# VectorE, ScalarE and GpSimd in the program's own order through the mixer of a hybrid decoder layer

## The chip, the core and the metric

The kernel runs on one NeuronCore of a Trainium2 chip. The metric is the device time of one execution in microseconds (us), lower is better. Engines are named as in the profile: PE (TensorE matmuls), PEld (its weight loads), DVE (VectorE), ACT (ScalarE), POOL (GpSimd) and SP (SyncE, which here only issues DMAs).

## The reference

One layer of 2048 channels on 256 tokens. After an RMSNorm, one wide projection gives the inputs of two branches: a gated DeltaNet (GDN, 8 heads of 128) and a block-sparse attention (MoBA, 8 heads of 128; with 256 tokens it is plain causal attention). Both are merged by sigmoid gates; an output projection and a gated MLP of width 5632 follow.

```python
h = rms_norm(x, ln1)
qkv_a, beta_a, decay_a, z_a, qkv_b, gate_a, gate_b = split_columns(h @ w_in)
# branch A: silu(causal conv of width 4) on q, k, v; l2norm of q and k;
# decay g, beta; per chunk of 64 tokens a triangular solve and the delta rule;
# rms_norm(o) * silu(z)
y_a = gated_deltanet(qkv_a, ...) @ w_branch_a
# branch B: rotary on a quarter of the head, causal softmax attention
y_b = moba_attention(rope(q_b), rope(k_b), v_b) @ w_branch_b
x = x + (sigmoid(gate_a) * y_a + sigmoid(gate_b) * y_b) @ w_out
u = causal_dwconv(rms_norm(x, ln2) @ w_up, ffn_conv, ffn_conv_bias)
x = x + (silu(u_gate) * u_val) @ w_down
out = rms_norm(x, final_norm)
```

## The kernel before

**Weights in two parts.** A float32 matrix product is made of three fp32r products: high part of the weights by the high part of h, high by low, low by high. A weight tile is 128 x 2048 float32 (1 MB, tile `wraw`, three buffers, loaded by SP in `fetch`). `split` (line 137) turns each half of 1024 columns into `wh` (a cast on ACT) and `wl` (a subtraction on DVE, line 134). `wh` and `wl` have four buffers each, so two tiles' worth. `pump` makes halves in program order as far as `due` allows; `take` hands the next tile to the matmuls; `gone` says which tiles the matmuls have been written out for, so that their buffers can be taken again.

**Main matmuls.** `chunk` gives 256 output columns of the projection: two tiles of 16 blocks, three matmuls of 256 columns each, so 96 matmuls of `main_mm` (line 123); a half is read by 24 of them. In each group of two heads (four groups) the chunks are GDN q, k, v and z (`delta`), MoBA q and k (`queries`), and in every second group one product for the values (`values_of`). Then come 16 chunks of gates, the branch products, the output projection, the MLP. The first q and k of GDN are made ahead, in the load phase (line 296).

**Turns.** After some 16 main matmuls (`EVERY`) `main_mm` calls `tick`, which advances every generator in `bg` to its next `yield`: that is a turn. The generators are `gdn` (norms, decay factors, the solve, the state), `moba` (rotary, scores, softmax, values) and `rotary` (sine and cosine tables). They mix small matmuls, DVE, ACT and POOL work, and DMAs through DRAM tiles (`dA`, `dC`, `dX`, `dE`) that POOL issues.

**Convolution.** `conv4` (from line 498) writes `un = ps * R1b` with `join` (line 239), where `un` has one buffer for all convolutions, then one ACT scaling for each of two heads (line 506), six DVE multiply-adds (line 508) and a SiLU. For the first k `conv4` gets `mid`, which writes out `decay()` (lines 460 to 484, the per-head decay and beta) and places the six multiply-adds of that k behind decay's last scan (line 480).

**Order.** The tile framework schedules the whole program with a timeline model: each engine's instructions are put in an order of the model's choosing, by readiness and priority. `tc.issue_after(ins)` queues work behind one instruction of its engine (`late()` queues behind the last `wl` written out), `tc.high_priority()` (in `join`) moves work ahead. On the chip each engine then works through its list.

Of the kernel before, what the change touches and what calls it, by code (L numbers as in the profile page):

```python
# [72 lines left out]
def layer_kernel(ctx: ExitStack, tc: tile.TileContext, w_first, xT, pos, cst, vec, convw, ffw, bdv,  # L73
# [40 lines left out]
    def take():  # L114
        n = taken[0]
        taken[0] += 1
        due[0] = 2 * n + 3
        passed[0] = 0
        pump()
        return n, made[2 * n:2 * n + 2]  # L120

    def main_mm(ps, a, b, start, stop):
        mark[0] = pe.matmul(ps, a, b, start=start, stop=stop, skip_group_check=True).ins  # L123
        passed[0] += b.free_size()
        if passed[0] >= 6144:
            due[0] = 2 * taken[0] + 2
            pump()
# [82 lines left out]
    def block(ps, j, w, x, kt, k0=0, k1=None, turn=False):  # L210
        for k in range(k0, k1 or kt):
            wh, wl = cut(w, (k + (j * kt if kt == H else 0)) * P, P)
            for w_, a in ((wh, 0), (wh, 1), (wl, 0)):
                main_mm(ps[:, j], w_, x.one(k, a, turn), j == k == a == 0 and w_ is wh,
                        k == kt - 1 and w_ is wl)

    def chunk(x, kt, name, steps=((0, 0, None), (1, 0, None)), c=None):
# [9 lines left out]
        for i, (j, k0, k1) in enumerate(steps):  # L227
            if j not in ws:
                ws[j] = take()
            block(ps, j, ws[j][1], x, kt, k0, k1, bool(again) and name in ("gdn", "z", "moba"))  # L230
            if kt != H and j not in [t[0] for t in steps[i + 1:]]:
                gone.add(ws[j][0])
        if kt == H:
            gone.add(ws[0][0])
# [162 lines left out]
    def rotary():  # L397
# [89 lines left out]
    def turned(rem):  # L487
        pt = sdt("pt_cols")
        for i in range(2):
# [3 lines left out]
        for i in range(2):  # L493
            pe.transpose(pt[:, 80 + 16 * i:96 + 16 * i], R1[:16, i * P:(i + 1) * P], ident[:16, :16])
        dve.tensor_copy(cols.rearrange("p a b -> p (a b)"), pt[:, :112])
        dve.tensor_scalar(cols[:, 0:2, :].rearrange("p a b -> p (a b)"), pt[:, :32], -1.0, None, op0=ALU.mult)

    left, early = [], []

    def conv4(t, ps, b0, to=None, mid=None):  # L500
# [11 lines left out]
        else:  # L512
            act.activation(to, t.rearrange("p j (b c) -> p j b c", c=64), AF.Silu)

# [18 lines left out]
    def gdn(h0, kq, v):  # L533
# [4 lines left out]
        yield from wait(2)  # L538
        pq = sdt("ssq")[:, :P]
        with tc.issue_after(mark[0]):  # L540
            for c, (i, j) in enumerate(((0, 0), (0, 1), (1, 0), (1, 1))):
                pe.matmul(pq[32 * c:32 * c + 32], ones[:, :32], sq[:, j, i * P:(i + 1) * P], start=True, stop=True,
                          skip_group_check=True)
        act.copy(sq[:, 0, :P], pq)
        st = gl.tile([P, 8, 4], F32, name="st")

        def exps():
            dve.tensor_tensor(gam[:, :, 0::2, :], gam[:, :, 0:2, :], nm[:, None, None, :].to_broadcast([P, 2, 2, P]), op=ALU.add)
            for j in range(2):
                c = 8 + h0 + j  # L550
                for q, a in enumerate((0, 2, 1)):
                    act.activation(gam[:, j, q, :], gam[:, j, q, :], AF.Exp, bias=cols[:, a, c:c + 1])

        if h0:
            exps()
        yield

        pq = sdt("ssq")[:, :P]
        pe.transpose(pq, sq[:, 0, :P], ident)
        dve.tensor_scalar(st[:, 0, :], pq[:, ::32], EPS, P * EPS, op0=ALU.add, op1=ALU.mult)  # L560
# [3 lines left out]
        yield from wait(2)  # L564
# [5 lines left out]
        for j in range(2):  # L570
            mmg(p1[:, j], three(kqh[:, 0, j, P:], kql[:, 0, j, P:], kqh[:, :, j, P:], kql[:, :, j, P:]))
        yield
        if left:
            turned(left.pop())
        jk = g.tile([P, P], F32, name="jk", bufs=1)
        for j in range(2):
            for i, d in ((0, p0[j][:, 0, :P]), (1, p1[:, j, 0, :])):
                with late():
                    diag = dve.scalar_tensor_tensor(jk, d, 1.0, ident, op0=ALU.mult, op1=ALU.mult,
                                                    accum_out=st[:, 1, 2 * i + j:2 * i + j + 1])  # L580
# [4 lines left out]
        if not h0:  # L585
            with tc.issue_after(diag.ins):
                exps()
        aq0 = gl.tile([P, 2, 2, T], F32, name="aq0")
        aq1 = gl.tile([P, 2, 2, P], F32, name="aq1")
        for j in range(2):  # L590
            gv = gam[:, j, 0:2, :].rearrange("p a b -> p (a b)")
            dve.scalar_tensor_tensor(aq0[:, j], p0[j], st[:, 3, j:j + 1], gv[:, None, :].to_broadcast([P, 2, T]),
                                     op0=ALU.mult, op1=ALU.mult)
        for j in range(2):
# [3 lines left out]
        for i in range(2):  # L598
            for b in range(2):
                pe.transpose(pvt[:, 2 * i + b, :], v[:, 2 * i + b, :], ident)  # L600
        dA = dr.tile([4, P + 1, P], F32, name="dA")
        pool.dma_start(dA[0:2, :P].rearrange("j s c -> s j c"), aq0[:, :, 0, :P])
        pool.dma_start(dA[2:4, :P].rearrange("j s c -> s j c"), aq1[:, :, 0, :])
        dC = dr.tile([16, 32, 32], F32, name="dC")
# [5 lines left out]
        X = g.tile([P, 160], F32, name="X", bufs=1)  # L610
        pool.tensor_copy(X, C["rows"])
        yield
        rt2 = gl.tile([P, 2, 2], F32, name="rt2")
        vb = gl.tile([P, 2, 2, P], F32, name="vb")
        with tc.issue_after(highs[-1].ins):
            for j in range(2):
                for b in range(2):
                    o = slice(64 * b, 64 * b + 64)
                    act.activation(rt2[64 * j:64 * j + 64, :, b], st[o, 1, j::2], AF.Sqrt, bias=epst[o])
            for i in range(2):  # L620
                for b in range(2):
                    act.mul(vb[:, i, b], pvt[:, 2 * i + b], rt2[:, i, b:b + 1])
        yield from wait(13)
# [14 lines left out]
        Xr = g.tile([P, 16, 16], F32, name="Xr", bufs=1)  # L638
        pool.dma_start(Xr.rearrange("p m c -> p (m c)"), dram(dX, 0, (256, 16), (0, 8), (1, 256)))
# [9 lines left out]
        for q in range(4):  # L649
            pool.dma_start(S1[32 * q:32 * q + 32, :, 32 * q:32 * q + 32],  # L650
                           dram(dA, q * 64 * (P + 1) + 32, (P, 32), (2 * (P + 1) * P, 2), (1, 32)))
        yield from wait(10)
        with late():
            rows(Xm, W, Xr, False)
        for j in range(2):
            pool.dma_start(S2[64 * j:64 * j + 64, :, 64 * j:64 * j + 64],
                           dram(dA, j * (P + 1) * P + 64, (P, 64), (2 * (P + 1) * P, 2), (1, 64)))
# [3 lines left out]
        early.append(h0)  # L661
        E = gl.tile([P, 2, 2, 32], F32, name="E", bufs=1)
        pool.dma_start(E.rearrange("p e i c -> p (e i) c"), dram(dE, 0, (32, P), (4096, 4), (1, 32)))
        yield from wait(3)
        for q in range(4):
            for b in range(2):
# [4 lines left out]
        with late():  # L671
            dve.transpose(Et, E[:, 0])
        yield from wait(2)
        py = r3(sdt("py")[:, :64], 32)
        for i in range(2):
            pe.matmul(py[:, i], S1[:, i], Et[:, i], start=True, stop=True)
        Y = gl.tile([P, 2, 4, 32], F32, name="Y", bufs=1)
# [4 lines left out]
        for i in range(2):  # L682
            pe.matmul(pu[:, i], Y[:, i].rearrange("p a b -> p (a b)"), E[:, 1, i], start=True, stop=True)
        for j in range(2):
# [10 lines left out]
        for i in range(2):  # L695
            p0_ = sdt("w0")[:, :P]
            pe.matmul(p0_, UB[:, i, 0], vb[:, i, 0], start=True, stop=True)
            w0 = gl.tile([P, P], F32, name="w0", bufs=1)
# [4 lines left out]
            pe.matmul(pz, S2[:, i], w0, start=True, stop=True)  # L703
            dve.tensor_tensor(vb[:, i, 1], vb[:, i, 1], pz, op=ALU.subtract)
            yield from wait(2)
            p1_ = sdt("w1")[:, :P]
            pe.matmul(p1_, UB[:, i, 1], vb[:, i, 1], start=True, stop=True)
            apart(i, 1, p1_)
            yield
            if i == 0:  # L710
                pr = r3(sdt("r1"), P)
                for j in range(2):
                    pe.matmul(pr[:, j, :], aq0[:, j, 0, P:], u[:, j, :], start=True, stop=True)
                for j in range(2):
# [6 lines left out]
        for j in range(2):  # L721
            pe.matmul(po[:, j, :], aq0[:, j, 1, :P], u[:, j, :], start=True, stop=True)
            mmg(po[:, 2 + j, :], [(aq0[:, j, 1, P:], u[:, j, :]), (aq1[:, j, 1, :], u[:, 2 + j, :])])
        ot = gl.tile([P, 4, P], F32, name="ot", bufs=1)
        for p in range(4):
            act.activation(ot[:, p], po[:, p], AF.Square, accum_out=st[:, 4, p:p + 1])
        yield from wait(3)
        with late():
# [386 lines left out]
```

## Time and profile before

| | us |
|---|---|
| median of 3 runs | 1450.16 (1449.38 to 1450.17) |
| the profiled execution | 1450.27 |
| its span, first to last instruction | 1448.5 |

| engine | busy us | share of the span |
|---|---|---|
| PE | 1434.0 | 99% |
| PEld | 1377.9 | 95% |
| DVE | 951.4 | 66% |
| ACT | 771.9 | 53% |
| POOL | 186.3 | 13% |

The profiled execution lies within the spread of the three runs, so sums against its trace can be read against the median. Matmuls overlap, and the end of each is modelled: PE's busy time is no measure of its free time. Its waits, the spacing of its matmuls and the granted clock are.

### The profile page before, as it was taken

The numbers are of one execution on the slowest core, as the hardware profiler recorded it, in microseconds if no ns is written. First come the engines' busy times: TensorE is split into PE (matmuls) and PEld (weight loads), VectorE is DVE, ScalarE is ACT, GpSimd is POOL, SyncE is SP. The second block draws the span as 40 slices with busy tenths as digits, with TensorE's granted clock in tenths as the row PEclk, the third lists the DMA queues.
The fourth block names the chain that finished last, engine by engine and source line by source line (L and its number), as shares of the span: only waits on it lengthen the run. The fifth ranks groups of instructions, "written<-read, shape, count | busy, mean of one in ns | idle before, by whom it ended". The sixth has DMA issues, their size and how long they took to land.

```text
span 1448.5 us, 26964 instructions
## 1 busy us (share of the span) xinstructions
PE 1434.0 (99%) x11268; PEld 1377.9 (95%) x11268; DVE 951.4 (66%) x1385; ACT 771.9 (53%) x1095; POOL 186.3 (13%) x236
## 2 busy tenths in 40 slices
PE   9999999999999999999999999999999999999998
PEld 9989998999999999999999999999999998888886
DVE  7879577686755546767776666666666676555454
ACT  7676575665746444444555555554554554444444
POOL 0030221222203000101131111111111110000000
PEclk9999999999999999999999999999999999999999
DMA  8575554555555565566585555555555555555552
GB/s 315 191 230 188 188 171 168 183 201 190 165 176 181 194 204 185 195 228 215 198 278 190 202 189 191 203 188 191 202 185 195 202 182 198 196 187 200 193 188 113
DMA packets 46458, 283.81 MB, mean 196 GB/s; under 512 B 7632, under 2 KB 8800, under 8 KB 14464
## 3 DMA queue, kind: packets, MB, share of 16 engines
q1 hardware_dynamic: 39344, 270.38, 53.9%
q0 software_dynamic: 6272, 9.61, 2.5%
q8 instruction: 88, 1.44, 0.4%
q10 hardware_dynamic: 720, 2.10, 0.4%
q14 instruction: 34, 0.28, 0.1%
HBM read 275.34 MB, written 3.82 MB: 193 GB/s over the span
## 4 chain that ended last, share of the span: by engine, by line
PE 98%; ACT 1%; issue 0%; POOL 0%; DVE 0%; ACTq 0%; POOLq 0%
PE ps_up L123 33%; PE pd L88 17%; PE ps_gate L123 12%; PE ps_gdn L123 7%; PE ps_moba L123 6%; PE ps_wo L123 6%; PE ps_br L123 6%; PE ps_v L123 3%; PE ps_z L123 3%; PE ps_gdn L296 2%; PE g L88 1%; PE warm L283 0%; PE sc L766 0%; PE py_b L794 0%; PE po L88 0%
## 5 line engine op out<-in xcount | busy, mean ns | idle before, releaser
L134 DVE TENSOR_TENSOR wl<-wraw,wh 128x1024 fp32r<-128x1024 f32 (+1 forms) x496 | 611.4, 1234 | 373.1 <-ACT wh L137 370.0
L137 ACT CAST wh<-wraw 128x1024 fp32r<-128x1024 f32 (+1 forms) x496 | 515.7, 1043 | 581.8 <-PE ps_up L123 196.1
L123 PE MATMUL ps_up<-h,wh 128*128 128x256 f32 x2816 | 479.2, 276 | 0.0
L123 PEld LDWEIGHTS ps_up<-h,wh 128*128 128x128 f32 x2816 | 423.8, 188 | 0.0
L123 PE MATMUL ps_up<-h,wl 128*128 128x256 f32 x1408 | 388.9, 276 | 0.0
L123 PEld LDWEIGHTS ps_up<-h,wl 128*128 128x128 f32 x1408 | 264.4, 188 | 0.0
L123 PE MATMUL ps_gate<-hc,wh 128*128 128x256 f32 x1024 | 178.8, 278 | 0.0
L123 PEld LDWEIGHTS ps_gate<-hc,wh 128*128 128x128 f32 x1024 | 155.2, 188 | 0.0
L123 PE MATMUL ps_gate<-hc,wl 128*128 128x256 f32 x512 | 142.4, 278 | 0.0
L88 PE MATMUL pd<-wl,ah 128*128 128x512 f32 x336 | 125.4, 389 | 0.0
L88 PE MATMUL pd<-wh,al 128*128 128x512 f32 x336 | 124.4, 389 | 0.0
L88 PE MATMUL pd<-wh,ah 128*128 128x512 f32 x336 | 115.5, 389 | 0.0
L979 POOL TENSOR_TENSOR acts<-sg,cvf 128x256 f32<-128x256 f32 x44 | 62.7, 1425 | 408.2 <-ACT sg L978 399.2
L123 PE MATMUL ps_gdn<-hc,wh 128*128 128x256 f32 x640 | 113.5, 280 | 0.0
L123 PEld LDWEIGHTS ps_gdn<-hc,wh 128*128 128x128 f32 x640 | 97.6, 188 | 0.5 <-issue 0.4
L123 PEld LDWEIGHTS ps_gate<-hc,wl 128*128 128x128 f32 x512 | 96.4, 188 | 0.0
L123 PE MATMUL ps_moba<-hc,wh 128*128 128x256 f32 x512 | 92.4, 283 | 0.0
L123 PE MATMUL ps_gdn<-hc,wl 128*128 128x256 f32 x320 | 89.5, 280 | 0.0
L123 PE MATMUL ps_wo<-mc,wh 128*128 128x256 f32 x512 | 87.1, 276 | 0.0
L123 PEld LDWEIGHTS ps_moba<-hc,wh 128*128 128x128 f32 x512 | 79.2, 191 | 0.5 <-issue 0.4
L123 PEld LDWEIGHTS ps_wo<-mc,wh 128*128 128x128 f32 x512 | 77.2, 188 | 0.0
L88 PEld LDWEIGHTS pd<-wh,al 128*128 128x128 f32 x336 | 63.1, 188 | 13.2
(464 smaller groups left out, 1974.2 us busy)
## 6 DMA issues: line engine op xcount, KB each, us to landing
wraw<-in_w_up SPq DMA_DIRECT2D x88, 1024.0 KB, 4.9
wraw<-in_w_dn SPq DMA_DIRECT2D x44, 1024.0 KB, 4.9
wraw<-in_w_gate SPq DMA_DIRECT2D x32, 1024.0 KB, 4.9
wraw<-in_w_gdn SPq DMA_DIRECT2D x28, 1024.0 KB, 5.2
wraw<-in_w_moba SPq DMA_DIRECT2D x16, 1024.0 KB, 4.9
wraw<-in_w_o SPq DMA_DIRECT2D x16, 1024.0 KB, 5.0
wraw<-in_w_mv SPq DMA_DIRECT2D x8, 1024.0 KB, 4.9
wraw<-in_w_ba SPq DMA_DIRECT2D x8, 1024.0 KB, 4.9
```

The costliest lines, as they stand in the source:

```text
L88: pe.matmul(ps, a, b, start=(start and i == 0), stop=(stop and i == n - 1), **kw)
L123: mark[0] = pe.matmul(ps, a, b, start=start, stop=stop, skip_group_check=True).ins
L134: return (eng or dve).tensor_tensor(lo, src, hi.bitcast(F32), op=ALU.subtract)
L137: highs.append(act.copy(hi, src))
L296: pe.matmul(ps_two[b // 2][:, b % 2], wv[t][:, k - a, b * P:(b + 1) * P], hc.one(k, x_), start=(k == t == x_ == b % 2 == 0), stop=(k == KD ...
L979: pool.tensor_tensor(acts[:, c, :], sg, t[:, 1, :], op=ALU.mult)
```

## The change

- Between GDN's first v chunk and the end of the gates, DVE, ACT and POOL issue their instructions in the order in which the program writes them out (`tc.manual_schedule`). PE and SP stay with the scheduler; so does everything written out ahead of the region (the first q and k, `decay`) and behind it, and so does the place where the region's instructions fall among those.
- `late()` and the other `issue_after` uses inside the region go away.
- Convolutions from the first v on use `conv_turns`: `join` into `un` at once, then the ACT scalings, the multiply-adds of each head and the SiLU in turns of their own. The SiLU of z and the sigmoid of the gates come one turn later (`soon`).
- `gdn`, `moba` and `rotary` are cut into smaller portions, with a `yield` between what one engine makes and what the next reads, and whole turns between dependent DMAs.
- `gone` counts halves and no longer tiles, and `due` is one half further ahead, in all stages that use `pump`.

The diff, cut to its core:

```diff
@@ pump, take, main_mm
-            if n > 1 and n - 2 not in gone:
+            if n > 1 and (n - 2, h) not in gone:
...
-        due[0] = 2 * n + 3
+        due[0] = 2 * n + 4
...
-            due[0] = 2 * taken[0] + 2
+            due[0] = 2 * taken[0] + 3
@@ block
+            if (o + P) % HALF == 0:
+                gone.add((n, o // HALF))
@@ new, beside conv4 (which stays for the first q and k)
+    def conv_turns(t, ps, b0, to=None):
+        un = g.tile([P, 2, T], F32, name="un", bufs=1)
+        join(un, ps, R1b)
+
+        def turns():
+            yield
+            for j in range(2):
+                act.activation(t[:, j, :], un[:, j, :], AF.Identity, scale=cwv[:, b0 + j, 3:4])
+            yield
+            for j in range(2):
+                w = cwv[:, b0 + j, :]
+                for d in (1, 2, 3):
+                    dve.scalar_tensor_tensor(t[:, j, d:], un[:, j, :T - d], w[:, 3 - d:4 - d], t[:, j, d:],
+                                             op0=ALU.mult, op1=ALU.add)
+                yield
+            if to is None:
+                act.activation(t, t, AF.Silu)
+            else:
+                act.activation(to, t.rearrange("p j (b c) -> p j b c", c=64), AF.Silu)
+
+        bg.append(turns())
@@ delta
             else:
+                if gr == 0:
+                    order_st.enter_context(tc.manual_schedule(engines={
+                        mybir.EngineType.DVE, mybir.EngineType.Activation, mybir.EngineType.Pool}))
                 ps = chunk(hc, KD, "gdn")
...
-                conv4(t, ps, 8 * a + h0,
-                      v.rearrange("p b (j c) -> p j b c", c=64))
+                conv_turns(t, ps, 8 * a + h0, v.rearrange("p b (j c) -> p j b c", c=64))
...
-        act.activation(yv, yv, AF.Silu)
+        soon(lambda: act.activation(yv, yv, AF.Silu))
@@ gdn: solve and its DMAs
-        yield from wait(13)
...
-            with late():
-                dve.tensor_tensor(tm[:, :, :, :i + 1], Xd[:, :, :, :i + 1],
-                                  Ad[:, :, None, :i + 1, i].to_broadcast([P, 2, 2, i + 1]), op=ALU.mult)
+            dve.tensor_tensor(tm[:, :, :, :i + 1], Xd[:, :, :, :i + 1],
+                              Ad[:, :, None, :i + 1, i].to_broadcast([P, 2, 2, i + 1]), op=ALU.mult)
...
-            if i % 4 == 3:
+            if i % 3 == 2:
                 yield
...
-        yield from wait(10)
-        with late():
-            rows(Xm, W, Xr, False)
+        yield
+        Xr = g.tile([P, 16, 16], F32, name="Xr", bufs=1)
+        pool.dma_start(Xr.rearrange("p m c -> p (m c)"), dram(dX, 0, (256, 16), (0, 8), (1, 256)))
+        yield from wait(5)
+        rows(Xm, W, Xr, False)
+        yield
...
+        yield from wait(2)
         E = gl.tile([P, 2, 2, 32], F32, name="E", bufs=1)
         pool.dma_start(E.rearrange("p e i c -> p (e i) c"), dram(dE, 0, (32, P), (4096, 4), (1, 32)))
...
-        yield from wait(6)
+        yield from wait(2)
         Et = gl.tile([P, 2, 32], F32, name="Et", bufs=1)
-        with late():
-            dve.transpose(Et, E[:, 0])
+        dve.transpose(Et, E[:, 0])
         yield from wait(2)
         py = r3(sdt("py")[:, :64], 32)
@@ moba
-        yield from wait(3)
+        yield from wait(4)
...
+        largest(0)
+        yield
+        largest(1)
+        yield
+        exps(0)
+        exps(1)
+        yield from wait(2)
+        share(0)
+        yield
+        share(1)
+        yield from wait(2)
@@ the end of the region, after the gates
     while bg:
         tick()
+    order_st.close()
```

The rest of the diff is of the same kind: more `yield`s between a small matmul and the instruction that reads its result, `values_of` reading a half of a tile at a time, `turned` cut into a PE and a DVE part, `st` with three buffers.

## Rows read from the trace of the kernel before

**Rows 1.** The page: engines; then shares of the chain that ended last.

```profile
PE 1434.0 (99%) x11268; PEld 1377.9 (95%) x11268; DVE 951.4 (66%) x1385; ACT 771.9 (53%) x1095; POOL 186.3 (13%) x236
PE 98%; ACT 1%; issue 0%; POOL 0%; DVE 0%; ACTq 0%; POOLq 0%
```

**Rows 2.** The chain in order of time: start us, length us, what.

```profile
31.80 10.72 PE ps_gdn L123 x94
42.52 10.92 PE ps_z L123 x96
...
449.51 98.01 PE ps_gate L123 x864
```

**Rows 3.** PE's waits: line, waited for, us in total, times, longest.

```profile
PE py L676 <- issue: 5.0, 2, 4.3
PE pot L738 <- ACT ot L733: 1.4, 1, 1.4
```

**Rows 4.** Stretches: PE, PEld, DVE, ACT, POOL busy (count), granted clock, DMA.

```profile
252.00:253.00 1.00, 0.00 (x0) 0.00 (x0) 1.00 (x3) 1.00 (x2) 1.00 (x3) 0.74 0.99 410
...
255.00:256.00 1.00, 1.00 (x6) 1.00 (x7) 0.94 (x2) 0.00 (x0) 1.00 (x3) 0.50 0.11 17
...
258.00:259.00 1.00, 1.00 (x7) 1.00 (x7) 0.75 (x1) 0.00 (x0) 0.00 (x0) 0.50 1.03 418
...
260.00:261.00 1.00, 1.00 (x11) 1.00 (x11) 0.28 (x1) 0.40 (x1) 0.00 (x0) 1.00 0.94 377
```

**Rows 5.** Timeline ahead of the long wait: start, us, instruction [idle before <-releaser].

```profile
239.02 0.53 POOL L639 DMA_DIRECT2D Xr<-dX  x1 [2.47 <-DMA dX<-X]
239.87 1.05 ACT L137 CAST wh<-wraw 128x1024 fp32r<-128x1024 f32 x1 [1.80 <-PE ps_moba L123]
244.29 1.08 DVE L643 TENSOR_TENSOR tw<-W,Xr 128x512 f32<-128x512 f32 x1 [5.44 <-DMA Xr<-dX]
245.28 1.23 DVE L134 TENSOR_TENSOR wl<-wraw,wh 128x1024 fp32r<-128x1024 f32 x1
250.37 0.78 POOL L663 DMA_DIRECT2D E<-dE  x1 [1.35 <-DMA dE<-X]
254.23 0.25 DVE L672 STREAM_TRANSPOSE Et<-E 128x64 f32<-128x64 f32 x1 [0.31 <-DMA E<-dE]
```

**Rows 6.** Timeline of DVE and ACT from the first convolutions to v's join.

```profile
41.36 1.21 DVE L134 TENSOR_TENSOR wl<-wraw,wh 128x1024 fp32r<-128x1024 f32 x1
45.91 0.69 DVE L239 TENSOR_TENSOR un<-ps_gdn,R 128x512 f32<-128x512 f32 x1
47.65 0.40 DVE L463 SCALAR_TENSOR_TENSOR nz<-gc 16x256 f32<-16x256 f32 x1
51.88 0.42 ACT L464 ACTIVATE ez<-nz 16x256 f32<-16x256 f32 x1
52.32 0.28 DVE L468 TENSOR_SCALAR den<-ez 16x256 f32<-16x256 f32 x1 [0.50 <-ACT ez L464]
...
54.99 1.23 DVE L134 TENSOR_TENSOR wl<-wraw,wh 128x1024 fp32r<-128x1024 f32 x1 [0.61 <-ACT wh L137]
...
64.36 1.21 DVE L134 TENSOR_TENSOR wl<-wraw,wh 128x1024 fp32r<-128x1024 f32 x1
...
66.59 0.84 DVE L508 SCALAR_TENSOR_TENSOR kq<-un,cwv,kq 128x255 f32<-128x255 f32 x2
71.83 0.47 DVE L508 SCALAR_TENSOR_TENSOR kq<-un,cwv,kq 128x253 f32<-128x253 f32 x1
72.33 0.69 DVE L239 TENSOR_TENSOR un<-ps_gdn,R 128x512 f32<-128x512 f32 x1
```

**Rows 7.** Groups between 30 and 450 us: busy us, mean ns | idle before.

```profile
L134 DVE TENSOR_TENSOR wl<-wraw,wh 128x1024 fp32r<-128x1024 f32 x135 | 164.5, 1221 | 66.3 <-ACT wh L137 63.4 <-PE ps_z L123 2.3
L630 DVE TENSOR_TENSOR tm<-X,Xa 128x8 f32<-128x8 f32 (+14 forms) x60 | 13.3, 221 | 0.8
L632 DVE TENSOR_REDUCE X<-tm 128x4 f32<-128x8 f32 (+14 forms) x60 | 11.3, 188 | 0.8
```

More of the change, by code (lines that the diff above doesn't have):

```diff
@@ L226, in chunk @@
                 pe.matmul(idle[:, :P], ws[0][1][0][0][:, :P], x.one(0, 0)[:, :P], start=True, stop=True)
-        for i, (j, k0, k1) in enumerate(steps):
+        for j, k0, k1 in steps:
             if j not in ws:
                 ws[j] = take()
[L230 to L234, printed above, removed]
+            block(ps, j, ws[j], x, kt, k0, k1, bool(again) and name in ("gdn", "z", "moba"))
         return ps
@@ L563, in gdn @@
         split(kqh, kql, kq)
-        yield from wait(2)
+        yield
+        pq = sdt("ssq")[:, :P]
+        for c, (i, j) in enumerate(((0, 0), (0, 1), (1, 0), (1, 1))):
+            pe.matmul(pq[32 * c:32 * c + 32], ones[:, :32], sq[:, j, i * P:(i + 1) * P], start=True, stop=True,
+                      skip_group_check=True)
+        yield
+        act.copy(sq[:, 0, :P], pq)
         p0 = []
@@ L584, in gdn @@
                           st[:, 3, :].rearrange("p (a b) -> p a b", b=2), cols[:, 3:5, h0:h0 + 2], op=ALU.mult)
-        if not h0:
-            with tc.issue_after(diag.ins):
-                exps()
+        for j in range(2):
+            c = 8 + h0 + j
+            for q, a in enumerate((0, 2, 1)):
+                act.activation(gam[:, j, q, :], gam[:, j, q, :], AF.Exp, bias=cols[:, a, c:c + 1])
+        yield from wait(2)
         aq0 = gl.tile([P, 2, 2, T], F32, name="aq0")
@@ L593, in gdn @@
                                      op0=ALU.mult, op1=ALU.mult)
+        rt2 = gl.tile([P, 2, 2], F32, name="rt2")
+        for j in range(2):
+            for b in range(2):
+                o = slice(64 * b, 64 * b + 64)
+                act.activation(rt2[64 * j:64 * j + 64, :, b], st[o, 1, j::2], AF.Sqrt, bias=epst[o])
+        yield
         for j in range(2):
@@ L600, in gdn @@
                 pe.transpose(pvt[:, 2 * i + b, :], v[:, 2 * i + b, :], ident)
+        yield
+        vb = gl.tile([P, 2, 2, P], F32, name="vb")
+        for i in range(2):
+            for b in range(2):
+                act.mul(vb[:, i, b], pvt[:, 2 * i + b], rt2[:, i, b:b + 1])
         dA = dr.tile([4, P + 1, P], F32, name="dA")
@@ L603, in gdn @@
         pool.dma_start(dA[2:4, :P].rearrange("j s c -> s j c"), aq1[:, :, 0, :])
+        X = g.tile([P, 160], F32, name="X", bufs=1)
+        pool.tensor_copy(X, C["rows"])
+        yield from wait(2)
         dC = dr.tile([16, 32, 32], F32, name="dC")
@@ L606, in gdn @@
             pool.dma_start(dC[8 * e:8 * e + 8], dram(dA, e * 32 * (P + 1), (64 * (P + 1), 8), (P, 32), (1, 32)))
+        yield from wait(2)
         Xa = g.tile([P, 33 * 32], F32, name="Xa", bufs=1)
         pool.dma_start(Xa[:, :1024], dram(dC, 0, (1024, 16), (0, 8), (1, 1024)))
+        yield from wait(4)
         pool.memset(r3(Xa, 33)[:, :, 0:1], -1.0)
[L610 to L622, printed above, removed]
-        yield from wait(13)
+        yield from wait(2)
         Xd = X.rearrange("p (e x) -> p e x", e=2)[:, :, :64].rearrange(
@@ L637, in gdn @@
         pool.dma_start(dX.rearrange("q (a r c) -> (q a) r c", r=2, c=16), X1)
-        Xr = g.tile([P, 16, 16], F32, name="Xr", bufs=1)
-        pool.dma_start(Xr.rearrange("p m c -> p (m c)"), dram(dX, 0, (256, 16), (0, 8), (1, 256)))
+        yield
+        for q in range(4):
+            pool.dma_start(S1[32 * q:32 * q + 32, :, 32 * q:32 * q + 32],
+                           dram(dA, q * 64 * (P + 1) + 32, (P, 32), (2 * (P + 1) * P, 2), (1, 32)))
         def rows(dst, w, a, neg):
@@ L726, in gdn @@
             act.activation(ot[:, p], po[:, p], AF.Square, accum_out=st[:, 4, p:p + 1])
-        yield from wait(3)
-        with late():
-            dve.scalar_tensor_tensor(st[:, 5, :], st[:, 4, :], 1.0 / P, st[:, 0, :], op0=ALU.mult, op1=ALU.add)
+        yield
+        dve.scalar_tensor_tensor(st[:, 5, :], st[:, 4, :], 1.0 / P, st[:, 0, :], op0=ALU.mult, op1=ALU.add)
+        yield
         act.activation(st[:, 6, :], st[:, 5, :], AF.Sqrt)
+        yield
         dve.reciprocal(st[:, 7, :], st[:, 6, :])
+        yield
         for p in range(4):
             act.mul(ot[:, p], po[:, p], st[:, 7, p:p + 1])
-        yield from wait(4)
+        yield from wait(2)
         pot = r3(sdt("pot"), T)
@@ L760, in moba @@
         each(lambda t, b, o: pool.dma_start(t, Xc[o, b]))
-        yield from wait(3)
-        py = r3(sdt("py_b"), T)
-        ss = []
+        yield from wait(4)
+        ss, pss, mxs = [], [], []
         for j in range(2):
@@ L787, in moba @@
             pe.transpose(pp[:, T:T + P], s_[:, P:T], ident)
+            pps.append(pp)
+        yield
+        for j in range(2):
             pT = m.tile([P, 3 * P], F32, name="pT_")
-            act.copy(pT, pp[:, :3 * P])
+            act.copy(pT, pps[j][:, :3 * P])
             ss[j] = pT
-            yield
+        yield from wait(2)
+        py = r3(sdt("py_b"), T)
         for j in range(2):
```

133 lines of the change are left out of this document (80 added, 53 removed).

## The prediction

> **What bounds the kernel now.** I read the page first. PE is busy for 99% of the span, and 98% of the chain that ended last is PE [rows 1]: in every stage the matmuls end last, and another engine costs time only where it makes PE wait. The chain in order of time gives the pace: 864 matmuls of the gates in 98.01 us are 113.4 ns each, the first v takes 10.72 us for 94 [rows 2], 114 ns. At that pace nothing is to be had; what can be had is PE's waits. PE's own waits between the first v and the gates are two on `py` (5.0 us together, one of them 4.3) and one on `pot` (1.4 us) [rows 3]. The stretches around 250 us show what the long one costs besides: the granted clock is 0.74 in the third microsecond of that wait and 0.50, the lower of its two levels (1.2 GHz), while PE works on; PE starts 6 to 7 matmuls per us there against 11 once the clock is 1.00 again [rows 4]. From 254.6 us, when PE goes on, to 260 that is 5.4 x (1 - 6.5/11) = 2.2 us. So 5.0 + 1.4 + 2.2 = 8.6 us, 0.6% of the time, is all that the region holds back.
>
> The timeline shows where the 4.3 us come from. DVE stands idle for 5.44 us until `Xr` has landed, then makes `Xm`; only then can POOL write `dE` and read `E`, which `Et` and `py` wait for [rows 5]. The order of PE had `py` too early for that.
>
> **The change, part by part.**
>
> *Old waits.* Per group the new portions put five turns between the issue of `Xr` and its reader, and six between the issue of `E` and `Et`. A turn is 16 matmuls, 16 x 0.1134 = 1.8 us, about 2.0 with the small matmuls in it. That is 10 and 12 us; `Xr` needed 5.3 us from issue to reader (239.02 to 244.29), `E` 3.9 (250.37 to 254.23) [rows 5]. DVE's wait there goes, and PE's waits on `py` with it; `pot` likewise follows its producer by two turns. Bounds: 0 (the order of PE, still the scheduler's, puts a small matmul too early again) to -8.6. I take -8.6, since each margin is about twice the row.
>
> *A new wait, at v's join.* The region begins with the first v. Its `conv_turns` writes out `join(un)` directly behind v's matmuls, ahead of z's first `take`. `un` has one buffer, held by the convolution of the first k, whose six multiply-adds stand behind `decay`'s last scan. In the trace v's join, ready when v's matmuls ended at 42.5 us [rows 2], runs at 72.33, right behind the last multiply-add of that k (71.83 + 0.47) [rows 6]: it waited 30 us, at no cost, because splits went past it. In program order nothing on DVE's list of the region goes past it. Which splits stand ahead of it? Ahead of the join `pump` has reached `due` = 7: halves 0 to 6, that is v's two tiles, z's first tile and the first half of z's second. Half 7 is written out by z's `take`, behind the join. PE needs its `wl` 72 matmuls into z: 42.5 + 72/96 x 10.92 [rows 2] = 50.7 us.
>
> When does the join run? Half 6 is split at 41.36 to 42.6 [rows 6], as before. From there DVE has only the first q's convolution, `decay` and the first k's convolution to do, all outside the region. `nz` ended at 48.05 with two splits since 42.6 ahead of it; without these (1.22 us each [rows 7]) at 45.6. `ez` followed 4.25 us later on ACT (48.05 to 52.30) behind two other pieces and a table load. With ACT's order unchanged that gives 49.9 us; 2 us earlier if ACT takes `ez` first. From `den` (52.32) to the end of the scans (66.59) 14.3 us passed, with five splits in between, first and last shown [rows 6], 6.1 us, and z's join, 0.7: 7.5 us are left. Then six multiply-adds at 0.42 [rows 6], 2.5; the join, 0.7; half 7, 1.2. Sum: 49.9 + 7.5 + 2.5 + 0.7 + 1.2 = 61.8, or 59.8 with the early `ez`. DVE's work alone, with no gap for `ez`, gives 45.6 + 7.5 + 2.5 + 1.9 = 57.5. PE therefore waits 6.8 to 11.1 us; I take 10.0, near the order that ACT had. A wait of this length is over twice the one in rows 4, so the clock falls in it too: +2.2. Together +12.2. Queued behind the waiting join are half 7, all later splits and v's multiply-adds; behind ACT's scalings of v (which read `un`) the casts of half 9 and on; PE waits for the first of these. After it DVE has h8 to h11 and v's multiply-adds to do in 7 us, about as long as PE takes for the halves in hand, so I add no second wait here.
>
> The Trainium skill, page "PSUM — Partial Sum Buffer", section "Engine vs sequencer instructions", says that the queues of ScalarE, VectorE and GpSimd are strictly first in, first out. The trace agrees: while DVE waited for `Xr` until 244.29, a half whose cast began at 239.87 and took 1.05 stood behind it and was split at 245.28 [rows 5]. Could a ready split pass a waiting join, the 12.2 us would be 0 and the sum 1443; I give that no chance of its own.
>
> *Later in the region.* A split is now written out 71 or 72 matmuls ahead of its use, 8.2 to 9 us; cast and split take 2.3, so DVE and ACT may run some 6 us behind PE's place in the program. Splits take 16/24 x 1.22 = 0.8 us of a turn of 2.0 [rows 7]. The densest stretch is the second group: there the solve (15 pairs of 0.41 us [rows 7], 6.1), q's convolution (0.7 + 2.5), k's join, both heads' scores and softmax of `moba`, and one `rows` (1.08 + 0.7 as for `Xm`, rows 5) fall into the same eight turns. The scores' and softmax' DVE part I estimate at 4.5 from its share of the groups. Sum 6.1 + 3.2 + 0.7 + 4.5 + 1.8 + 8 x 0.8 = 22.7 us in 16: 6.7 us behind, at the limit. One bound is 0, the other about 3 us (ACT's exponentials and SiLU come in one turn there) plus 2.2 of clock, 5. I take 1.5, nearer to 0 because the sum barely exceeds the limit. The first, third and fourth groups stay below it, as no convolution, or no `moba`, meets the solve there.
>
> *No cost.* Splits one half further ahead change nothing for PE in the gates, the branches and the MLP, where it already goes at 113.4 ns; DVE is at 66% of the span [rows 1], and if that cover went, PE would wait for single halves. DMAs keep number and size; POOL, at 13% [rows 1], waits for them in order without anyone behind it within two turns.
>
> **Sum.** Against the profiled execution's 1450.27 us: -8.6 + 12.2 + 1.5 = +5.1, 1455.4. That execution is 0.1 us from the median, so no correction. I say 1455.
>
> **The rivals.**
>
> - *The join costs nothing* (faster): only if the first k's convolution ends by 49 us, 8 us ahead of the sum of DVE's work, or `un` gets its buffer otherwise. Then 1450.3 - 8.6 + 1.5 = 1443. For: all that work lies outside the region, so the scheduler is free to hurry it. Against: the single buffer and the scans are data dependences. 15%.
> - *The old waits stay beside the new one* (slower still): PE's order is again made on modelled times, and small matmuls meet late results, this time of engines that run in order; the clock falls each time. 1450.3 + 12.2 + 1.5 = 1464. For: `Xr`'s landing was late once already. Against: the added turns. 15%.
> - *In-order engines fall behind in every group*, not in the second alone: from the point where DVE is over 6 us behind, each group adds about 3 + 2.2 us; three groups more than the forecast 15.6: 1471. Against: the same sum of work per turn in other groups stays 2 to 3 us below the limit. 7%.
> - *The region does little*: the scheduler's order was near the program's, and a short join wait and a part of the old waits cancel, 1450. For: PE is 99% busy either way. 8%.
>
> **How the numbers follow.** The forecast, 1455, has 55% and spreads by its bounds: the join's wait 6.8 to 11.1, the second group 0 to 5, i.e. 1450.5 to 1460. The range takes in part of the first and second rival: 1443.5 to 1464. A change of 0.2%, 2.9 us, is about what a measurement of this kernel can tell from none. Faster (below 1447.4): 15% + 2% = 0.17. Within (to 1453.2): the 8% and some 15% of the forecast's lower end, 0.23. Slower: the rest, 0.60.
>
> **What would show it.** Right: a gap of PE in z's second tile near 51 us that ends with half 7's split, right behind v's join and the first k's last multiply-add, and a granted clock of 0.50 behind it; no wait on `py` near 250; `Xr`'s reader without idle time ahead of it. The second group's step: splits that end shortly before PE needs them around 55 + 150 us. Wrong: v's join before 50 us, or half 7 ahead of it in DVE's list; PE gaps elsewhere in the region.

## The result and the profile after

The changed kernel takes 1472.35 us (1471.23 to 1473.35), the kernel before 1449.66 in the same comparison: a ratio of 1.0156, 95% interval 1.0141 to 1.0171. That is 22.7 us slower where 5 were predicted, and above the predicted range, which ended at 1464.

The page of the changed kernel, its engines and the shares of the chain that ended last, beside [rows 1]:

```profile
PE 1445.3 (98%) x11268; PEld 1388.5 (94%) x11268; DVE 962.7 (65%) x1385; ACT 766.6 (52%) x1092; POOL 186.7 (13%) x236
...
PE 95%; DVE 3%; ACT 2%; issue 1%; POOL 0%; ACTq 0%; DVEq 0%; POOLq 0%
```

PE still ends last, but 5% of the chain is now DVE and ACT, which had 1% of it. PE's waits (line, waited for, us in total, times, longest), beside [rows 3]:

```profile
PE ps_z L123 <- DVE wl L134: 13.1, 2, 11.7
PE ps_gdn L123 <- ACT wh L137: 2.2, 1, 2.2
```

The waits on `py` and `pot` are gone, and one of 11.7 us stands in z, for a `wl`, as predicted. The timeline there, first a cast of ACT and then DVE (start, length, instruction, idle time before it and who ended it), beside [rows 6]:

```profile
42.56 1.05 ACT L137 CAST wh<-wraw 128x1024 fp32r<-128x1024 f32 x1 [1.70 <-PE ps_gdn L123]
...
50.37 0.28 DVE L470 TENSOR_SCALAR den<-ez 16x256 f32<-16x256 f32 x1 [4.31 <-ACT ez L466]
...
57.68 0.73 DVE L482 TENSOR_TENSOR_SCAN gc<-ones,gt 16x128 f32<-16x128 f32 x2
...
59.30 1.65 DVE L517 SCALAR_TENSOR_TENSOR kq<-un,cwv,kq 128x254 f32<-128x254 f32 x4
61.05 0.69 DVE L239 TENSOR_TENSOR un<-ps_gdn,R 128x512 f32<-128x512 f32 x1
61.66 2.35 DVE L134 TENSOR_TENSOR wl<-wraw,wh 128x1024 fp32r<-128x1024 f32 x2
```

It is the order that the prediction wrote down: the scans, the first k's multiply-adds, v's join, half 7. No split runs between 42.6 and 61.7 us. PE in the stretches around it (PE's busy time, matmuls, granted clock, DMA share, GB/s), beside [rows 4], and two of its matmuls there:

```profile
55.00:62.00 7.00, 0.00 (x0) 0.50 0.02 5
63.00:68.00 5.00, 5.00 (x23) 0.50 0.90 274
68.00:69.00 1.00, 1.00 (x9) 0.84 0.62 213
...
63.31 0.63 PE L123 MATMUL ps_z<-hc,wh 128*128 128x256 f32 x2
...
63.95 0.63 PE L123 MATMUL ps_z<-hc,wh 128*128 128x256 f32 x2
```

PE goes on at the lower level, 1.2 GHz, from 62.9 to 68 us. The matmuls shown repeat after three, so three take 63.95 - 63.31 = 0.64 us, 213 ns each, where 113.4 is the pace. (The counts of a stretch can't be used for this, as they take in matmuls that reach over its ends.) That costs 5.1 x (1 - 113.4/213) = 2.4 us. Wait and clock make 14.1.

The other loss is nowhere in the waits. Both kernels have idle matmuls (`kick`): at the start of a few chunks `chunk` writes out three matmuls of 128 columns whose result nobody reads. The chain in order of time, from those of gate chunk 7 to those of the up projection, beside [rows 2]:

```profile
460.29 0.28 PE kick L230 x3
460.57 10.94 PE ps_gate L123 x96
471.51 0.44 PE pot L788 x4
471.95 90.45 PE ps_gate L123 x768
562.40 90.45 PE ps_br L123 x768
652.86 90.45 PE ps_wo L123 x768
743.31 8.36 PE ps_up L123 x71
...
755.05 0.28 PE kick L230 x3
755.33 44.73 PE ps_up L123 x394
```

Up to the four `pot` matmuls it goes at 10.94/96 = 114.0 ns each, behind them at 90.45/768 = 117.8, and from the next idle matmuls on at 44.73/394 = 113.5 again. Nothing waits, and the granted clock is 1.00 in both. Before, the gates ran at 113.4 from 449.5 us on [rows 2]. Three times 768 matmuls by 4.4 ns are 10.1 us, and the 71 of the up projection add 0.3. At chunk 7 the changed kernel is 460.57 - 449.51 = 11.1 us late; so about half of the loss came in the region and half behind it.

### The profile page after: what moved, and what is told of

Its sections match the earlier page's. It is cut to its first block, busy times and chain, and to the rows that moved or that the text cites. A ratio compares the mean times of both kernels' runs of the same rounds, so it can differ in the third digit from the quotient of the medians.

```text
span 1470.5 us, 26967 instructions
## 1 busy us (share of the span) xinstructions
PE 1445.3 (98%) x11268; PEld 1388.5 (94%) x11268; DVE 962.7 (65%) x1385; ACT 766.6 (52%) x1092; POOL 186.7 (13%) x236
## 4 chain that ended last, share of the span: by engine, by line
PE 95%; DVE 3%; ACT 2%; issue 1%; POOL 0%; ACTq 0%; DVEq 0%; POOLq 0%
PE ps_up L123 33%; PE pd L88 16%; PE ps_gate L123 12%; PE ps_br L123 6%; PE ps_wo L123 6%; PE ps_moba L123 6%; PE ps_gdn L123 5%; PE ps_v L123 3%; PE ps_z L123 2%; PE ps_gdn L296 2%; DVE wl L134 1%; PE g L88 1%; DVE kq L536 0%; ACT wh L137 0%; DVE kq L517 0%
## 5 line engine op out<-in xcount | busy, mean ns | idle before, releaser
L123 PE MATMUL ps_wo<-mc,wh 128*128 128x256 f32 x512 | 90.5, 281 | 0.0
```

## Experiments

The kernel before gave 1450.2 to 1450.5 us beside each group of runs below; ratios are against it.

**Idle matmuls in the gates.** Four kernels change only the chunks at which the three idle matmuls stand.

```diff
-KICKS = {"gate": (7,), "up": (1, 23)}
+KICKS = {"gate": (10,), "up": (1, 23)}      # a_kick10
+KICKS = {"gate": (), "up": (1, 23)}         # a_nokick, and b_nokick from the kernel before
+KICKS = {"gate": (7, 10), "up": (1, 23)}    # a_kick7_10
```

At chunk 10:

> The changed kernel with the three idle matmuls of the gates at the start of chunk 10 instead of 7, behind the last small matmuls of the GDN portions, nothing else. Theory 1 (PE goes at 117.8 ns a matmul from 480 to 743 us because small matmuls came after those idle matmuls, and would go at 113.3 ns behind idle matmuls that come after the last small matmul): 113.3 ns from about 490 us on, the time falls by some 10 us, to about 1462. Rival (the slow pace comes from the halves made one half further ahead or from another order of the splits, and the idle matmuls have no part in it): pace 117.8 ns in the later gates as before, the time within 3 us of 1472.

1462.88 us, ratio 1.0084 (1.0069 to 1.0099): 9.5 us less than the changed kernel, as theory 1 has it. But its chain shows that the pace came back before the idle matmuls:

```profile
458.77 13.19 PE ps_gate L123 x112
471.96 0.44 PE pot L788 x4
472.40 21.78 PE ps_gate L123 x192
494.18 0.28 PE kick L230 x3
494.46 65.34 PE ps_gate L123 x576
559.80 87.04 PE ps_br L123 x768
```

117.8 ns ahead of `pot`, 113.4 behind it, on both sides of the idle matmuls. The same four matmuls that had slowed PE now made it quick. So the reason was in doubt, and two more kernels were run.

> The changed kernel without the idle matmuls in the gates. With those at chunk 10 the pace was 117.8 ns up to the last small matmuls (pot, 471.7 us) and 113.4 ns from there on, ahead of the idle matmuls at 494 us; in the changed kernel the same four pot matmuls took the pace from 113.4 to 117.8 ns. Theory A (a burst of small matmuls decides between two self-sustaining paces, by where it meets them; the idle matmuls at chunk 7 only made pot meet the quick one): without any idle matmuls pot again leaves 113.4 ns and the time is that of the idle matmuls at chunk 10, 1462 to 1464. Theory B (the idle matmuls must come last to restore the pace): 117.8 ns to 743 us, 1471 to 1473.

1463.09 us, 1.0085 (1.0070 to 1.0100): theory A. Without any idle matmuls in the gates the 112 matmuls ahead of `pot` take 13.19 us and the 768 behind it 87.06.

> The changed kernel with idle matmuls at gate chunk 7, as it has them, and again at chunk 10. PE is expected at 117.8 ns from 471.7 us to 494 us, behind pot, as in the changed kernel. If idle matmuls at a chunk's start restore the pace, 113.3 ns from 494 us on, and the time is 1463 to 1464 (1472 less 250 us x 4.5/117.8 = 9.5, plus 0.3). If they don't, 117.8 ns up to 743 us and 1472.

1462.60 us, 1.0082 (1.0067 to 1.0097). Here `pot` comes, as in the changed kernel, behind idle matmuls and slows PE (22.61 us for 192), and those at chunk 10 restore it (65.34 for 576). So idle matmuls can restore the quick pace; but those at chunk 7 were of no use, since a burst came after them, and without them the burst itself happened to leave the quick pace.

> The kernel before without the three idle matmuls in the gates, nothing else. Theory 1 (the idle matmuls are what brings PE back to 113.3 ns a matmul after the last small matmuls): PE goes at 117.8 ns from 449 us to the kick in the second chunk of the up projection near 735 us, about 2500 matmuls by 4.4 ns, so 8 to 12 us slower than the kernel before, 1458-1462. Rival (the pace follows from the weights' order in the stage and returns by itself once the small matmuls end): no change, 1450.

1449.84 us, 0.9994 (0.9984 to 1.0003): the rival. In the kernel before PE is quick ahead of `pot` and behind it, with no idle matmuls:

```profile
438.56 10.78 PE ps_gate L123 x95
449.35 0.44 PE pot L738 x4
449.78 97.96 PE ps_gate L123 x864
```

A burst of small matmuls can thus turn the pace either way or leave it. In the free order below the same four `pot` matmuls leave the slow pace slow (13.19 us for the 112 ahead of them, 22.61 for the 192 behind). What decides is open.

**A second `un`.**

```diff
-        un = g.tile([P, 2, T], F32, name="un", bufs=1)
+        un = g.tile([P, 2, T], F32, name="un", bufs=2)
```

> The changed kernel with a second buffer for un, nothing else. Theory 1 (the predicted wait: v's join waits for the buffer that the first k's convolution still reads, and half 7 stands behind it on DVE): PE's stall of 11.9 us near 51 us and the clock of 0.50 behind it go, so the time falls by 10 to 14 us, to about 1459-1462. Rival (DVE and ACT are late there because all their work is in program order, whatever the join waits for): half 7 stays late behind the scans, PE still stalls by at least 8 us near 51 us, and the time stays within 3 us of 1472.

1470.99 us, 1.0140 (1.0125 to 1.0155): 1.4 us gained, which is not clear of noise. PE's waits, the first lines:

```profile
PE ps_moba L123 <- DVE wl L134: 3.8, 1, 3.8
PE ps_moba L123 <- ACT wh L137: 3.4, 1, 3.4
...
PE ps_z L123 <- DVE wl L134: 1.3, 1, 1.3
```

The long wait in z is down to 1.3 us, so the buffer was its cause. But two new ones, in the chunk behind z, with a low clock behind each, eat the gain. They end at 69.5 and 87.0 us, and the timelines of DVE and ACT name what held them:

```profile
61.24 2.64 DVE L476 SCALAR_TENSOR_TENSOR pv<-pv,s 16x256 f32<-16x256 f32 x6
...
68.28 1.21 DVE L134 TENSOR_TENSOR wl<-wraw,wh 128x1024 fp32r<-128x1024 f32 x1
...
82.50 0.23 ACT L445 ACTIVATE cs__957<-ang 128x32 f32<-128x32 f32 x1 [8.82 <-DVE ang L443]
```

The first split stands behind 7 us of work on DVE without a gap, `decay` and the first k's multiply-adds. The second wait is for casts, which stand behind the rotary's sine on ACT, and ACT stands idle 8.8 us for the sine's angle. Both theories are half right: the wait fell, the time did not.

> Both edits at once: second buffer for un, idle matmuls at gate chunk 10. If the two terms are separate causes they add: about -12 and -10 us, 1472 to some 1449-1451, as fast as the kernel before. If the pace is lost again by other events once the stall at 51 us is gone, only one of the two gains is seen: 1459 to 1462.

1461.48 us, 1.0073 (1.0058 to 1.0088): 1.4 less than with the later idle matmuls alone, again with intervals that overlap. The two edits add up; the second `un` is worth no more here.

**Program order taken away, wholly or from the front.** All three with the idle matmuls at chunk 10.

```diff
-                if gr == 0:
+                if gr == 1 and a == 0:     # a_g1_kick10; gr == 2: a_g2_kick10
                     order_st.enter_context(tc.manual_schedule(engines={
                         mybir.EngineType.DVE, mybir.EngineType.Activation, mybir.EngineType.Pool}))
```

In the free-order kernel the three lines are left out.

> The changed kernel with idle matmuls at chunk 10, and the region of program order beginning with the second group's first chunk (about 100 us) instead of the first v. Theory (the stall near 51 us, and those that took its place with a second un, come from decay and the first k's convolution standing ahead of everything in lists that are worked off in order): no PE wait above 2 us before 100 us, no clock of 0.50 there, 12 to 15 us less than with the idle matmuls at chunk 10 alone (1462.9): 1448 to 1451. Rival (the portions and the convolution in turns cost the time there, whatever the order): 1458 to 1463.

1455.85 us (its runs spread over 1453.2 to 1460.9), 1.0042 (1.0027 to 1.0057): 7.0 less, between the two. No low clock and no wait above 2 us is left ahead of 100 us, but PE waits 5.4 us for `wl` at 108, 118 and 140 us, the first two close behind the place where the list now begins. DVE's timeline there:

```profile
109.93 0.17 DVE L668 TENSOR_TENSOR tm<-X,Xa 128x8 f32<-128x8 f32 x1 [7.99 <-POOL Xa L661]
110.01 1.22 DVE L134 TENSOR_TENSOR wl<-wraw,wh 128x1024 fp32r<-128x1024 f32 x1
```

The solve's first step waits 8 us for `Xa`, and the split behind it waits too.

> The changed kernel with idle matmuls at chunk 10 and program order only from the third group's first chunk (about 180 us) on. With the region from the second group PE stalled at 108 and 118 us (5.1 us) and at 140 to 146 us (3.7 us). If program order costs only where its list begins and where solve and scores meet in the second group: 1447 to 1449, the free order's time within 1.5 us. If each entry into program order costs (the scheduler's tail of earlier work stands ahead of the list's first splits): 1452 to 1455.

1448.78 us, 0.9988 (0.9979 to 0.9997): the first theory. From the third group on program order costs 1.3 us against the free order of the next run, and the two intervals overlap.

> The changed kernel with idle matmuls at chunk 10 and without program order anywhere: the new portions, halves one half further ahead, the scheduler's order on all engines. If program order costs in later groups too (the stalls near 148 and 235 us, where DVE's list waits for scores), this is 2 to 5 us faster than the run with the region from the second group on. If program order is what removed the old waits on py and pot, they come back here (up to 8 us) and this is slower than that run.

1447.51 us, 0.9982 (0.9972 to 0.9991). PE's waits:

```profile
PE sc L815 <- DMA qk<-Xc: 3.4, 1, 3.4
...
PE py L717 <- issue: 0.6, 1, 0.6
```

Program order costs 1462.88 - 1447.51 = 15.4 us, and it was not what removed the old waits: the new portions do that in the scheduler's order as well (`py` 0.6, no `pot`). Portions and halves together gain 2.7 us; they were not run apart.

**The order without the portions.** The three lines of the region put into the kernel before, nothing else.

> The kernel before with its own portions, halves and convolutions, but VectorE, ScalarE and GpSimd in program order from the first v to the gates: the order alone, without the new portions. Prediction from the mechanism seen (in a list every instruction that waits holds up the splits behind it, and the old portions put a reader one turn or less behind its producer in several places): stalls of PE in every group, at least 20 us more than the kernel before, above 1475. Rival (the portions are not needed, order alone costs the 15 us that separate the changed kernel from its free order): 1460 to 1470.

1559.06 us, 1.0752 (1.0735 to 1.0768): the theory, and far beyond its 20 us. PE waits in every group, most for `wh`:

```profile
PE ps_z L123 <- ACT wh L137: 21.3, 4, 17.6
PE ps_gdn L123 <- ACT wh L137: 20.5, 7, 6.2
```

All the other edits of the change together, the smaller portions among them, save 1559.06 - 1472.35 = 87 us of what the order alone costs. This run also shows idle matmuls that do not give the quick pace. Here `pot` stands right ahead of those of gate chunk 7:

```profile
550.07 0.53 PE L226 MATMUL kick<-hc,wh 128*128 128x128 f32 x3
...
551.19 0.40 PE L123 MATMUL ps_gate<-hc,wh 128*128 128x256 f32 x2
...
553.66 0.40 PE L123 MATMUL ps_gate<-hc,wh 128*128 128x256 f32 x2
```

The two main matmuls shown are 21 apart, and 553.66 - 551.19 = 2.47 us make 117.6 ns each. So it goes until PE has to wait at 556 us; behind that wait it is quick.

**The scores' reader.** In the changed kernel DVE and ACT stand idle ahead of the second group's late splits. ACT's timeline:

```profile
144.67 1.28 ACT L540 ACT_TABLE_LOAD   x1 [8.27 <-DVE kq L536]
...
149.67 1.97 ACT L137 CAST wh<-wraw 128x1024 fp32r<-128x1024 f32 x2
```

and DVE's:

```profile
136.29 1.22 DVE L134 TENSOR_TENSOR wl<-wraw,wh 128x1024 fp32r<-128x1024 f32 x1
141.76 0.56 DVE L823 TENSOR_TENSOR s__1581<-sc,ct 128x384 f32<-128x384 f32 x1 [4.26 <-PE sc L816]
```

DVE's list has the softmax' first step one turn behind the scores, but PE, whose order is the scheduler's, does the scores later. The convolution's multiply-adds and splits wait behind that step; ACT's SiLU waits for these, and exponentials and casts for ACT.

```diff
             pss.append(ps)
-        yield
+        yield from wait(4)
```

> The changed kernel with idle matmuls at chunk 10, and the softmax' first DVE step four turns behind the scores' matmuls instead of one. Theory (in the list's order DVE stood 4.3 us idle for the scores with splits behind them, and the casts behind ACT's exponentials came late, so PE stalled 0.8 + 2.3 + 0.6 us between 144 and 151 us and 1.6 + 0.9 us near 237 us): most of these 6.2 us go, 1457 to 1459. Rival (DVE and ACT simply have too much work in these turns, whatever they wait for): the stalls move by some us and the time stays at 1462 to 1463.5.

1455.94 us, 1.0038 (1.0024 to 1.0051): 6.9 less than with the later idle matmuls alone, the theory, and a little more than the 6.2 that it summed. PE's waits are down to the one in z and the one before the region:

```profile
PE ps_z L123 <- DVE wl L134: 12.5, 2, 11.7
```

The work in these turns is the same, so it was the wait in the list and not the amount of work.

**What holds the first group.** Three kernels on top of that one: a second `un`, the first k's multiply-adds no longer behind decay's scans, and both.

```diff
-        with tc.issue_after(mid()) if mid else nullcontext():
+        if mid:
+            mid()
+        with nullcontext():
```

> The run with the later softmax step (1455.9) with a second un. In the changed kernel the second un moved the stall from 51 us to 65 and 83 us and gained 1.4 us; there, ACT's SiLU of the first k waited 7.9 us for decay and the first k with casts queued behind it. If that is the cause, again about 1 us is gained: 1454 to 1456. If the second group's scores hid the gain of the second un before: 1444 to 1447.

1455.10 us, 1.0034 (1.0021 to 1.0048): waits of 3.8 and 3.9 us in the chunk behind z again, 0.8 us gained. The second group had hidden nothing.

> The run with the later softmax step (idle matmuls at chunk 10, program order from the first v on; 1455.9, only the stall of 11.9 us near 51 us left), with the first k's multiply-adds no longer queued behind decay's last scan. In DVE's list the join of v then stands behind six multiply-adds and sv instead of behind all of decay. Theory (the stall is the time by which the chain decay, first k, join is late, as the prediction summed it): from the rows of the changed kernel, ez at 50.3, reciprocal to 52.4, sv 52.9, with multiply-adds in between, join and half 7 end at about 56 instead of 62.8, so PE waits some 5 us instead of 11.9; 7 us of wait and up to 2.2 us of low clock go: 1447 to 1449. Rival (as with the second un: DVE and ACT owe the same work, so the stall comes back some 15 us later): no less than 1454.

1456.05 us, 1.0040 (1.0028 to 1.0053). The wait in z is 4.4 us, as the theory summed it, and the time is the rival's. ACT's timeline shows what came next:

```profile
81.90 0.23 ACT L445 ACTIVATE cs__957<-ang 128x32 f32<-128x32 f32 x1 [11.64 <-DVE ang L443]
...
85.33 1.97 ACT L137 CAST wh<-wraw 128x1024 fp32r<-128x1024 f32 x2
```

ACT now stands 11.6 us in front of the rotary's sine, two casts behind it, and PE waits 2.9 us for them near 84 us; the granted clock falls to 0.50 behind each wait.

> Both: first k's multiply-adds not behind decay's scans, and a second un. If the chain was the whole cause and the buffer only its first place, nothing in front of v's join waits any longer: no PE wait above 2 us near 51 us, no low clock there, 1443 to 1445, below the kernel before. If the order in itself costs (DVE's list short of time for splits while decay runs): a stall of 2 to 5 us stays and the time is 1446 to 1450.

1454.36 us, 1.0030 (1.0019 to 1.0040), above both theories. In front of v's join nothing waits, but PE waits 3.0 us for two `wl` near 56 and 68 us and 3.6 for a `wh` behind the same sine. So the chain is not the whole cause either: with each blocker taken away the next instruction of a list that waits holds up the splits, and only 1.6 of the 8.4 us that separate this group of runs from the free order were found. The sine hardly moves: it runs at 85.1 us in the changed kernel, at 82.5 with two `un`, at 81.9 with the first k freed and at 80.7 with both, each time with casts behind it in the list. The scheduler's order has it at 95.6 us in the kernel before and at 101.1 in the free order. Whether the sine is the last blocker was not tried.

**The best version.** The free order, with the scores two turns later.

```diff
         each(lambda t, b, o: pool.dma_start(t, Xc[o, b]))
-        yield from wait(4)
+        yield from wait(6)
```

> The free-order kernel (new portions, idle matmuls at chunk 10, no program order; 1447.5) with the scores two turns later behind the DMAs of the rotated q and k, which PE waited 3.4 us for near 117 us. If only that wait held it back: 3 to 4 us less, 1443.5 to 1445. If the scheduler puts the scores where it likes, whatever the turn they are written in, the time stays at 1447.

1446.53 us, 0.9975 (0.9964 to 0.9985), 0.25% faster than the kernel before. The wait of 3.4 us is gone, but PE now waits 4.6 us in small pieces of at most 1.4 for splits and `py`, and the time is nearer to the rival's 1447. Against the free order the 1.0 us is not clear of noise, as the intervals overlap, and pace plays into it: here `pot` gave the quick one (21.78 us for the 192 matmuls behind it, 22.61 in the free order).

## Why the prediction was wrong

*Direction and new wait: right.* PE stopped at 51.2 us (predicted 50.7), the join ran at 61.05 (59.9), half 7 was split by 62.9 (61.8), the wait took 11.7 us (10.0) and the clock 2.4 (2.2): 14.1 for 12.2. The sum of its order had been 61.8 - 50.7 = 11.1, and 10.0 was taken below it; the rest lies in its first terms: `den` followed `ez` at 50.4 where 49.9 was taken, and the scans lost another half microsecond. The 2.2 us for the clock came out by luck. The counts of [rows 4] take in matmuls that reach over the ends of a stretch: at 113.4 ns 8.8 start in a microsecond, not 11, and at 213 ns 4.7. The low clock ended near 259.2 us and not at 260, and the two errors cancel. The Trainium skill's rule that the queues of ScalarE, VectorE and GpSimd are strictly first in, first out (page "PSUM — Partial Sum Buffer", section "Engine vs sequencer instructions") is borne out again: the cast of half 7 ended at 43.6 us and DVE stood idle for 4.3 us up to 50.4, yet its split ran at 61.7, behind the join.

*One cause for that wait: too simple.* The prediction named the single `un`. With two the wait in z fell to 1.3 us, and with the first k out of decay's chain to 4.4; the time gained 1.4 us and nothing. The prediction looked for the one instruction that waits longest. In a list worked off in order, several wait, and the later ones show only when PE is no longer late: ACT's sine ran 2.6 us earlier with two `un` (82.5 for 85.1 us), where the wait in z had shrunk by 10.4.

*Old waits: right, and by the cause named.* They are gone by the portions, as the free order shows, and not by the order. Yet portions and halves gained 2.7 us where 8.6 were taken: in the free order PE waits 3.4 us for the scores, at a granted clock of 0.50 from 122 to 124 us, and 0.6 for `py`, and the 304 gate matmuls around `pot` go at the slow pace, 1.3 us more.

*Later in the region: mis-sized.* 1.5 us was taken, the bound was 5; a later softmax step gave back 6.9. PE also stood idle for some 2 us near 237 us, in the third group, which the prediction held free. The step added up DVE's work per turn and compared it with the time of a turn. It had the place right, the second group, but not the reason: DVE stood idle for 4.3 us there, and ACT for 8.3. What was missing is that PE's order stays the scheduler's, so that a reader which stands one turn behind its producer in the program can stand ahead of it on the chip.

*No cost: the step that failed.* "Splits one half further ahead change nothing for PE in the gates, the branches and the MLP, where it already goes at 113.4 ns" looked for waits only. The trace shows 117.8 ns a matmul from 472 us to the up projection's 71 matmuls at 743, 10.4 us by its rows, and moving or leaving out the idle matmuls gave 9.3 to 9.8. What the change did was to move the last small matmuls, `pot`, which the kernel before has right ahead of the idle matmuls of gate chunk 7 and of its 864 undisturbed matmuls [rows 2], one chunk later, to 471 us, where they met the quick pace behind the idle matmuls and ended it. The portions moved them, not the order: in the free order too they stand at the start of chunk 8, and with the order alone ahead of chunk 7's idle matmuls. The kernel before held two hints. `chunk` puts matmuls into the gates that compute nothing, and the prediction did not ask what for. And its trace has the slow pace in short pieces:

```profile
428.62 2.71 PE ps_gate L123 x23
...
730.08 2.94 PE ps_up L123 x25
733.03 0.28 PE kick L226 x3
```

The first is 117.8 ns each, the second 117.6, and ended by idle matmuls. So "at that pace nothing is to be had" held for the rows that the prediction took and not for all of the region.

The four terms, with what the chip gave when each was taken away in turn:

| term | predicted | taken away |
|---|---|---|
| pace behind the gates' small matmuls | 0 | 1472.35 to 1462.88: 9.5 |
| second and third group, scores read too early | 1.5 | to 1455.94: 6.9 |
| the rest of program order, by the waits mostly the first group | 12.2 | to 1447.51: 8.4 |
| portions and halves, old waits | -8.6 | against 1450.2: -2.7 |

The third is less than the 14.1 us that PE loses near 51 us, since the free order has the wait of 3.4 us for the scores, which program order did not have. The rivals: the one in which in-order engines fall behind in every group named the time, 1471, by luck. The fourth group had no stall, those of the second and third came mostly from a reader that waits in the list, and 9.5 us of the time lie where no engine waits.

## What to carry to other kernels

Before an engine is set to program order, list for each instruction of its list that waits on another engine or a DMA what stands behind it; put readers as many turns behind as the producer's engine may reorder, and try where the order begins: here it cost 1.3 us from the third group on and 15.4 from the first v on. When one such wait is removed, look for the next in the same list before counting the gain. Where matmuls are all that is left, compare their spacing in long stretches as well as the waits: a few per cent can go without any idle time.

## What the runs showed of the hardware

PE has two paces for the same stream of weight loads and matmuls of 256 columns at a granted clock of 1.00, and keeps either for hundreds of microseconds. In the slow one the loads of `wh` differ; these loads in the gates between 500 and 560 us (duration in ns: least, median, most), first of the changed kernel, then of the one without idle matmuls in the gates:

```profile
L123 PEld LDWEIGHTS ps_gate<-hc,wh x340: 187/190/192, 499.9 to 559.8; 128*128 128x128 f32 x170
```

```profile
L123 PEld LDWEIGHTS ps_gate<-hc,wh x354: 187/188/188, 499.8 to 559.9; 128*128 128x128 f32 x177
```

In the slow stretch the loads of `wh` reach 192 ns, in the quick one none exceeds 188. Half of these loads are the longer ones (median 190), so the loads grow by some 4 ns on every third matmul, while the spacing grows by 4.4 on every one: the loads mark the slow pace, and the rows don't show that they cause it. Bursts of small matmuls can switch between the two. Behind three idle matmuls of 128 columns at the start of a chunk PE was quick within a few matmuls each time but one, in the kernel with the order alone, where `pot` stood right ahead of them; in the kernel before it stood there too, and PE was quick. The Trainium skill, page "TensorE: Matmul & The Clock Gate", section "Back-to-back issue gap", says that in such a stream the spacing is set by the weight load and the matmul together; the rows agree so far, as load and spacing change together.
